# A decoder layer on one core: fixed product order, list turns in two more sequences, a four-bank LayerNorm start, the second norm one group later, and a shared ending

## Chip, cores and metric

The kernel runs on one core of a Trainium2 chip. The metric is the device time of one execution in microseconds (us), the median of several runs; lower is better.

## What is computed

One layer of a decoder over 256 prompt positions and 8 x 4 sample positions, 288 rows in all, which share every weight. In float32, width 2048:

```python
h = rmsnorm(x, norm1_g)
proj = h @ w_in + b_in                     # 2048 -> 3072: a, gate, z
u = a * sigmoid(gate)                      # 1024 channels
c = silu(layernorm(depthwise_causal_conv(u_ext, conv_w, conv_b), ln_g, ln_b))   # 31 taps
d = multiscale_pool(z_ext)                 # 4 groups of 256, windows 2, 4, 8, 16, less z
p = (d @ pool_w, group by group) * pool_scale
x = x + concat[c, p] @ w_out               # 2048 -> 2048
f = square(relu(rmsnorm(x, norm2_g) @ w_ff1))   # 2048 -> 8192
x = x + f @ w_ff2
y = rmsnorm(x, norm_f)                     # also returned: the last 30 u and 15 z of each sequence
```

## The kernel before

Channels lie on the 128 partitions, so a row block is a 128 x 288 tile and x is 16 such tiles (xT). Every weight and every activation is split into a high and a low part of a reduced float32 form, and a product of two blocks is three TensorE products: high x high, weight-low x high, high x activation-low. ScalarE rounds a raw weight tile (wr) to whi (L265, 128 x 1024, a "half" of a block), and the rest, wlo, is made in a way that the table WAYS names for each stage: on VectorE (V, L270), on GpSimd (G, L273), or by an accumulating transfer (D). Five such split tiles are held at once.

gemm (L315) accumulates into PSUM: usually two banks of one 128 x 576 tile (ac, two in use at once), with two k tiles at a time, six products for each bank. 16 k tiles into two banks are 96 products, 8 are 48. The argument classes reorders the head of a gemm: each character asks for the next product in which (k + part) is even or odd. TURN is such a list of 48 characters. between puts small products ahead of a given k tile.

The order of the work: SEQUENCE lists the 16 steps that follow norm 1. c0 to c7 are the column blocks of the convolution (its two gate and value blocks, then sigmoid, then 31 taps on VectorE, L434, at low priority), p3 to p0 the pooled groups (eviction tz L457, window sums on GpSimd, L466 to L475, then dx, L477 and L478), and P3 to P0 the products of a pooled group with its pool_w (tile pp, 12 products), evicted by L489 and L490 into dx again. c0 and c1 run together in four banks; the row sums of norm 1 come near their end, and the row of inverse roots is spread over the partitions in c2. Then come eight W_out column groups over the pooled half (dx), in which the LayerNorm's mean (pmean), sums and row spread are placed, and eight over the convolved half (mx), which ScalarE and VectorE make pair by pair (L564 to L570). After each, x is updated (L559, L580) and the MLP's input ax is made (L596, L597) with its squares summed on GpSimd (ss2, L604). The MLP runs in four chunks: eight groups of w_ff1, eight of w_ff2. Inverse roots come from rsqrt_sums (three one-column products that put row sums on 96 partitions, then steps on 96 x 3 elements) and spread (three products with the identity). At the end the last x tiles are squared and summed the same way, VectorE scales the 16 tiles of xT by the row in six pieces (L652), and SyncE sends each piece out (L653).

The program is written in this order, and a scheduler that models the engines in time orders the instructions of each engine by it; tc.issue_after holds following instructions of the same engine behind a given one. Weights are split one gemm ahead (ready, weights). The lists before the change:

```python
SEQUENCE = "c0 c1 c2 c3 c4 p3 c5 p2 P3 c6 p1 P2 p0 P1 c7 P0"
TURN = "110100" * 4 + "01" * 6 + "1100" * 3
```

TURN is used in c2 (behind 36 alternating places), in the third W_out group of each half, and in the third group of the MLP's first chunk.

## Time and profile before

| | |
|---|---|
| median of 3 runs | 1087.61 us (1087.12 to 1087.72) |
| profiled execution, own time | 1087.97 us |
| its span, first to last instruction | 1086.2 us |
| TensorE / VectorE / ScalarE / GpSimd busy | 99% / 58% / 44% / 17% |
| mean granted TensorE clock | 0.997 |
| HBM read / written | 185.16 MB / 4.28 MB |

The profile comes from one execution. A busy time is the sum over an engine's instructions; PE is TensorE's products, PEld its weight loads, DVE VectorE, ACT ScalarE, POOL GpSimd, SP SyncE. PE also counts products that overlap in the pipeline, and the profile records each product of 288 columns once. The small products with float32 operands are recorded as two.

### The profile page before, as it was taken

Reading aid. Unit: us, or ns where it says so; the run is one execution under the profiler, and the core shown is the slowest. Engines: PE = TensorE matmul, PEld = TensorE weight load, DVE = VectorE, ACT = ScalarE, POOL = GpSimd, SP = SyncE. Lnnn points to the kernel's source line nnn. Section 1 sums busy time; section 2 is a strip of 40 time slices with the busy share of each in tenths; the row PEclk is TensorE's granted clock in tenths of the full one; section 3 lists DMA queues with packets and bytes.
Section 4 is the critical chain, followed back from the end, with each engine's and each line's share of the span. In section 5 each row is a group of like instructions: output and inputs, shape, how many; then the busy total and the mean of one; then the engine's idle time right before and its main releaser. Section 6 shows DMA issues by size and latency. Waiting matters only on the chain.

```text
span 1086.2 us, 19609 instructions
## 1 busy us (share of the span) xinstructions
PE 1073.7 (99%) x8206; PEld 1071.4 (99%) x8206; DVE 634.0 (58%) x813; ACT 477.9 (44%) x583; POOL 182.7 (17%) x212
## 2 busy tenths in 40 slices
PE   9999999999999999999999999999999999999996
PEld 8999999999999999999999999999999999999996
DVE  7899999678555444445454444545544445554553
ACT  8654445475544433334443333444433334444441
POOL 0888989613000000000000000000000000000000
PEclk9999999999999999999999999999999999999998
DMA  9896467545455555555555555555555555555522
GB/s 333 281 269 177 136 178 245 183 153 178 159 171 169 164 172 174 166 167 173 167 167 172 172 165 168 175 167 165 174 169 165 172 173 165 167 174 166 168 76 88
DMA packets 58120, 190.71 MB, mean 176 GB/s; under 512 B 6192, under 2 KB 11312, under 8 KB 58032
## 3 DMA queue, kind: packets, MB, share of 16 engines
q1 hardware_dynamic: 56480, 185.27, 52.2%
q0 software_dynamic: 1008, 3.67, 1.9%
q8 instruction: 64, 1.05, 0.4%
q10 hardware_dynamic: 544, 0.52, 0.1%
q14 instruction: 24, 0.20, 0.0%
HBM read 185.16 MB, written 4.28 MB: 174 GB/s over the span
## 4 chain that ended last, share of the span: by engine, by line
PE 96%; DVE 1%; ACT 1%; DMA 1%; issue 1%; POOL 0%; DVEq 0%
PE ac L315 95%; DMA wr<-in_w 1%; PE pp L315 0%; DVE xT L652 0%; ACT whi L265 0%; DVE wlo L270 0%; POOL wlo L273 0%; PE idle L233 0%; ACT n L567 0%; PE pt L250 0%; PE pt L230 0%; DVE z_all L391 0%; ACT z_all L389 0%; ACT hx L340 0%; DVE n L564 0%
## 5 line engine op out<-in xcount | busy, mean ns | idle before, releaser
L265 ACT CAST whi<-wr 128x1024 fp32r<-128x1024 f32 (+1 forms) x341 | 356.6, 1046 | 558.4 <-PE ac L315 540.4
L270 DVE TENSOR_TENSOR wlo<-wr,whi 128x1024 fp32r<-128x1024 f32 (+1 forms) x295 | 362.9, 1231 | 350.3 <-ACT whi L265 350.3
L315 PE MATMUL ac<-ax,whi 128*128 128x288 f32 x2048 | 351.5, 292 | 0.0
L315 PE MATMUL ac<-fx,whi 128*128 128x288 f32 x2048 | 350.1, 292 | 0.0
L315 PEld LDWEIGHTS ac<-ax,whi 128*128 128x128 f32 x2048 | 296.2, 187 | 0.0
L315 PEld LDWEIGHTS ac<-fx,whi 128*128 128x128 f32 x2048 | 295.6, 187 | 0.0
L315 PE MATMUL ac<-ax,wlo 128*128 128x288 f32 x1024 | 217.4, 292 | 0.0
L315 PE MATMUL ac<-fx,wlo 128*128 128x288 f32 x1024 | 216.3, 292 | 0.0
L315 PEld LDWEIGHTS ac<-ax,wlo 128*128 128x128 f32 x1024 | 162.7, 187 | 0.0
L315 PEld LDWEIGHTS ac<-fx,wlo 128*128 128x128 f32 x1024 | 162.2, 187 | 0.0
L315 PE MATMUL ac<-hx,whi 128*128 128x288 f32 x768 | 136.3, 295 | 0.6 <-DVE hx L338 0.6
L315 PEld LDWEIGHTS ac<-hx,whi 128*128 128x128 f32 x768 | 113.8, 188 | 1.0 <-ACT whi L265 0.8
L273 POOL TENSOR_TENSOR wlo<-wr,whi 128x512 fp32r<-128x512 f32 x78 | 105.9, 1411 | 32.7 <-ACT whi L265 30.4
L434 DVE SCALAR_TENSOR_TENSOR pc<-u_all,vec,pc 128x256 f32<-128x256 f32 x232 | 99.8, 483 | 3.0 <-ACT pc L431 1.6
L315 PE MATMUL ac<-hx,wlo 128*128 128x288 f32 x384 | 86.1, 296 | 0.3 <-DVE wlo L270 0.2
L315 PEld LDWEIGHTS ac<-hx,wlo 128*128 128x128 f32 x384 | 62.7, 188 | 1.1 <-DVE wlo L270 0.9
L315 PE MATMUL ac<-dx,whi 128*128 128x288 f32 x256 | 46.1, 296 | 0.0
L315 PE MATMUL ac<-mx,whi 128*128 128x288 f32 x256 | 45.2, 294 | 0.1
L617 DVE SCALAR_TENSOR_TENSOR t<-ac,r 128x576 f32<-128x576 f32 x32 | 24.2, 758 | 26.3 <-PE ac L315 25.2
L315 PEld LDWEIGHTS ac<-mx,whi 128*128 128x128 f32 x256 | 37.5, 188 | 0.6 <-ACT mx L569 0.3
L315 PEld LDWEIGHTS ac<-dx,whi 128*128 128x128 f32 x256 | 38.0, 188 | 0.1
L646 DVE TENSOR_TENSOR xT<-xT,ac 128x576 f32<-128x576 f32 x24 | 18.1, 754 | 19.4 <-PE ac L315 19.4
(108 smaller groups left out, 502.9 us busy)
## 6 DMA issues: line engine op xcount, KB each, us to landing
wr<-in_w SPq DMA_DIRECT2D x335, 512.0 KB, 3.6
wlo<-in_w POOLq DMA_DIRECT2D x7, 512.0 KB, 7.3
xT<-in_xT SPq DMA_DIRECT2D x7, 288.0 KB, 6.6
out_u_out<-u_all SPq DMA_DIRECT2D x1, 1208.0 KB, 9.7
out_yT<-xT SPq DMA_DIRECT2D x2, 576.0 KB, 2.9
u_all<-in_hist_c SPq DMA_DIRECT2D x8, 136.0 KB, 5.2
wr<-in_w SPq DMA_DIRECT2D x4, 256.0 KB, 3.3
out_z_out<-z_all SPq DMA_DIRECT2D x1, 668.0 KB, 8.2
```

The costliest lines, as they stand in the source:

```text
L265: nc.scalar.copy(hi, raw)
L270: nc.vector.tensor_tensor(lo, raw, f32(hi), op=ALU.subtract)
L273: nc.gpsimd.tensor_tensor(lo[:, j : j + 2, :], raw[:, j : j + 2, :], f32(hi[:, j : j + 2, :]), op=ALU.subtract)
L315: last = nc.tensor.matmul(banks[m][:, :T], gets[k // 8](k % 8, m)[w], rhs[k][x], start=j == ends[m][0], stop=j == ends[m][1])
L434: nc.vector.scalar_tensor_tensor(out=dst, in0=up[:, w : w + SEQ], scalar=cwv[:, w : w + 1], in1=pc, op0=ALU.mult, op1=ALU.add)
L617: nc.vector.scalar_tensor_tensor(out=t, in0=bk[:, :, :T], scalar=0.0, in1=both(r2), op0=ALU.max, op1=ALU.mult)
L646: nc.vector.tensor_tensor(x2, x2, bk[:, :, :T], op=ALU.add)
```

## The change

- **Order.** chain holds the last product; through mm every product from the end of the first gemm up to the third MLP group is issued behind it. P1 moves behind c7. TURN is also used in c5 and c7, and in the second instead of the third W_out group of the first half.
- **Norm 1 and start.** The spread of norm 1's row in c2 stands 12 products later. The first vector transfer goes ahead of x, and the second weight tile is sent after ScalarE's first table load.
- **LayerNorm.** The mean's products stand two k tiles earlier in their group. The first two W_out groups of the second half run as one gemm over four banks, whose two weight blocks are prepared together.
- **Second norm.** Its sums are two products of the split ss2 with a constant matrix, which leave the mean on all partitions; the inverse root is taken on 128 x 288 elements. It stands in the second MLP group instead of behind the first, and the first group is evicted after it.
- **End.** ScalarE takes the root straight from the sums; four VectorE steps follow. The row is spread twice: VectorE scales 12 tiles from the first in PSUM, ScalarE copies the second, and GpSimd scales 4 tiles one by one. Transfers alternate between SyncE and ScalarE.

Lines that are only "..." are left out:

```diff
-SEQUENCE = [(_s[0], int(_s[1])) for _s in "c0 c1 c2 c3 c4 p3 c5 p2 P3 c6 p1 P2 p0 P1 c7 P0".split()]
+SEQUENCE = [(_s[0], int(_s[1])) for _s in "c0 c1 c2 c3 c4 p3 c5 p2 P3 c6 p1 P2 p0 c7 P1 P0".split()]
+TURNS = ("c5", "c7")
...
-        queue.dma_start(raws[-1][:, :, k % 2 : k % 2 + n, :], src[:, :, k % 8 : k % 8 + n, :])
+        queue.dma_start(raws[k // 2][:, :, k % 2 : k % 2 + n, :], src[:, :, k % 8 : k % 8 + n, :])
...
-    for k in range(2):
-        first_weights(k, 1, nc.scalar)
+    first_weights(0, 1, nc.scalar)
+    nc.sync.dma_start(vec[:, 0:NG], io["vec"][:, 0:NG])
...
-        if k == 0:
-            nc.sync.dma_start(vec[:, 0:NG], io["vec"][:, 0:NG])
-        elif k > 1:
+        if k > 1:
...
+    first_weights(1, 1, nc.scalar)
...
-    def rsqrt_sums(parts, scale, after=None, busy=(0, 0)):
+    means = const.tile([P, P], F32R, name="means")
+    nc.vector.tensor_scalar(means, ones, DC / D, None, op0=ALU.mult)
+    cst = const.tile([P, 32], F32, name="cst")
+    eps, mean_d = cst[:, 0:1], cst[:, 1:2]
+    nc.vector.memset(eps, EPS)
+    nc.vector.memset(mean_d, 1.0 / D)
+    def inverse_root(mean, root, y, out):
+        nc.vector.reciprocal(y, root)
+        nc.vector.scalar_tensor_tensor(out=root, in0=mean, scalar=EPS, in1=y, op0=ALU.add, op1=ALU.mult)
+        nc.vector.scalar_tensor_tensor(out=root, in0=root, scalar=-0.5, in1=y, op0=ALU.mult, op1=ALU.mult)
+        nc.vector.scalar_tensor_tensor(out=out, in0=root, scalar=1.5, in1=y, op0=ALU.add, op1=ALU.mult)
+    def rsqrt_sums(parts, scale, after=None):
...
-        idle = cvp.tile([P, 512], F32, name=nm("idle"), tag="cv") if sum(busy) else None
...
-                last = nc.tensor.matmul(pt[:TB, j : j + 1], t[:, j * TB : (j + 1) * TB], ones[:, 0:1], start=n + j == 0, stop=n == len(parts) - 1 and j == 2)
-            with tc.issue_after(last.ins):
-                for j in range(busy[n] if n < 2 else 0):
-                    nc.tensor.matmul(idle[:, 0:P], ones, ones, start=True, stop=True)
+                last = mm(pt[:TB, j : j + 1], t[:, j * TB : (j + 1) * TB], ones[:, 0:1], start=n + j == 0, stop=n == len(parts) - 1 and j == 2)
...
-            last = nc.tensor.matmul(pr[:, j * TB : (j + 1) * TB], s[:, j : j + 1].to_broadcast([TB, P]), ident, start=j == 0, stop=j == 2)
+            last = mm(pr[:, j * TB : (j + 1) * TB], s[:, j : j + 1].to_broadcast([TB, P]), ident, start=j == 0, stop=j == 2)
...
-    def rsqrt_rows(*args):
-        return spread(rsqrt_sums(*args))[0]
...
-    def gemm(banks, rhs, m_outer=False, between={}, classes=""):
+    chain = []
+    def mm(*args, **kw):
+        with tc.issue_after(chain[-1]) if chain else nullcontext():
+            last = nc.tensor.matmul(*args, **kw)
+        if chain:
+            chain[0] = last.ins
+        return last
+    def gemm(banks, rhs, m_outer=False, between={}, classes="", singly=False):
...
-        gets = ready.pop()
-        step = 2 if len(banks) == 2 else 1
-        pairs = [(k, m) for k in range(0, n, step) for m in range(len(banks))]
+        gets = ready.pop(0)
+        units = [(k, 2) for k in range(0, n, 2)]
+        if singly:
+            units = [(k, 1) for k in range(n)]
+        pairs = [(k, width, m) for k, width in units for m in range(len(banks))]
...
-            pairs.sort(key=lambda km: km[1])
-        if step == 2:
-            parts = ((0, 0, 0), (1, 0, 0), (0, 1, 0), (1, 1, 0), (1, 0, 1), (0, 0, 1))
-        else:
-            parts = ((0, 0, 0), (0, 0, 1), (0, 1, 0))
-        todo = [(k + d, m, w, x) for k, m in pairs for d, w, x in parts]
+            pairs.sort(key=lambda p: p[2])
+        parts = {1: ((0, 0, 0), (0, 0, 1), (0, 1, 0)), 2: ((0, 0, 0), (1, 0, 0), (0, 1, 0), (1, 1, 0), (1, 0, 1), (0, 0, 1))}
+        todo, begins = [], {}
+        for k, width, m in pairs:
+            if m == 0:
+                begins[len(todo)] = k
+            todo += [(k + d, m, w, x) for d, w, x in parts[width]]
...
-            if j % (len(banks) * len(parts)) == 0:
-                ahead = between[k]() if k in between else None
-            with tc.issue_after(ahead.ins) if ahead is not None else nullcontext():
-                last = nc.tensor.matmul(banks[m][:, :T], gets[k // 8](k % 8, m)[w], rhs[k][x], start=j == ends[m][0], stop=j == ends[m][1])
+            if begins.get(j) in between:
+                ahead = between[begins[j]]()
+            with tc.issue_after(ahead.ins) if ahead is not None and not chain else nullcontext():
+                last = mm(banks[m][:, :T], gets[k // 8](k % 8, m)[w], rhs[k][x], start=j == ends[m][0], stop=j == ends[m][1])
...
-        for _ in range(8):
+        a, b = split(load()), split(load())
+        yield [lambda k, m: (a, b)[m // 2](k, m % 2)]
+        for _ in range(6):
...
-    with tc.issue_after(gemm(pair0 + pair1, hx, between={15: first_sums})):
-        third = conv_products(2, between={2: first_rows}, classes="01" * 18 + TURN)
+    chain.append(gemm(pair0 + pair1, hx, between={15: first_sums}, singly=True))
+    third = conv_products(2, between={4: first_rows}, classes="01" * 15 + TURN)
...
-            conv_pair(i, conv_products(i))
+            conv_pair(i, conv_products(i, classes=TURN if f"c{i}" in TURNS else ""))
...
-        nc.tensor.matmul(norm["mean"], ones, sum_c[:, 0, :], start=True, stop=False)
-        return nc.tensor.matmul(norm["mean"], ones, cs[-1][:, 1, :], start=False, stop=True)
+        mm(norm["mean"], ones, sum_c[:, 0, :], start=True, stop=False)
+        return mm(norm["mean"], ones, cs[-1][:, 1, :], start=False, stop=True)
...
-    BETWEEN = {5: {4: ln_mean}, 6: {6: ln_sums}, 7: {2: ln_rows}}
-    behind = nullcontext()
+    BETWEEN = {5: {2: ln_mean}, 6: {6: ln_sums}, 7: {2: ln_rows}}
...
-        with behind:
-            last = gemm(each(bk), [mixp[k] for k in korder], between=BETWEEN.get(g, {}), classes=TURN if g == 2 else "")
-        behind = tc.issue_after(last) if g > 3 else nullcontext()
+        gemm(each(bk), [mixp[k] for k in korder], between=BETWEEN.get(g, {}), classes=TURN if g == 1 else "")
...
     for g in range(8):
-        bk = bank2()
-        gemm(each(bk), mixc, classes=TURN if g == 2 else "")
+        if g == 0:
+            joint = [bank2(), bank2()]
+            gemm(each(joint[0]) + each(joint[1]), mixc, classes="01" * 24 + TURN)
+        bk = joint[g] if g < 2 else bank2()
+        if g > 1:
+            gemm(each(bk), mixc)
...
-    r2 = row("r2")
-    ssf = row("ssf")
+    rows2 = []
+    def second_rows():
+        hl = actp.tile([P, 4, T], F32R, name="hl", tag="act")
+        hi, lo = hl[:, 1, :], hl[:, 0, :]
+        nc.scalar.copy(hi, ss2)
+        nc.vector.tensor_tensor(lo, ss2, f32(hi), op=ALU.subtract)
+        bk, r2 = ms("mean2"), row("r2")
+        mean, root = bk[:, 0, :T], bk[:, 1, :T]
+        mm(mean, means, hi, start=True, stop=False)
+        last = mm(mean, means, lo, start=False, stop=True)
+        nc.scalar.activation(root, mean, AF.Sqrt, bias=eps)
+        inverse_root(mean, root, r2, r2)
+        rows2.append(r2)
+        return last
     for ch in range(DFF // FCH):
-        fx = []
+        fx, done = [], []
...
-            gemm(each(bk), x1, classes=TURN if ch == 0 and g == 2 else "")
-            if ch == 0 and g == 0:
-                nc.scalar.copy(r2, rsqrt_rows([ss2], 1.0 / D))
-            t = tmpp.tile([P, 2, T], F32, name=nm("t"), tag="ag", bufs=2)
-            nc.vector.scalar_tensor_tensor(out=t, in0=bk[:, :, :T], scalar=0.0, in1=both(r2), op0=ALU.max, op1=ALU.mult)
-            f = tmpp.tile([P, 2, T], F32, name=nm("f"), tag="ag2", bufs=2)
-            nc.scalar.activation(f, t, AF.Square)
-            fh, fl = act2("fx")
-            nc.scalar.copy(fh, f)
-            nc.vector.tensor_tensor(fl, f, f32(fh), op=ALU.subtract)
-            fx += halves((fh, fl))
+            gemm(each(bk), x1, between={2: second_rows} if ch == 0 and g == 1 else {}, classes="01" * 6 + TURN if ch == 0 and g == 1 else "")
+            if ch == 0 and g == 2:
+                chain.clear()
+            done.append(bk)
+            if ch or g:
+                for bk in done:
+                    t = tmpp.tile([P, 2, T], F32, name=nm("t"), tag="ag", bufs=2)
+                    nc.vector.scalar_tensor_tensor(out=t, in0=bk[:, :, :T], scalar=0.0, in1=both(rows2[0]), op0=ALU.max, op1=ALU.mult)
+                    f = tmpp.tile([P, 2, T], F32, name=nm("f"), tag="ag2", bufs=2)
+                    nc.scalar.activation(f, t, AF.Square)
+                    fh, fl = act2("fx")
+                    nc.scalar.copy(fh, f)
+                    nc.vector.tensor_tensor(fl, f, f32(fh), op=ALU.subtract)
+                    fx += halves((fh, fl))
+                done = []
         last = ch == DFF // FCH - 1
...
+                        ssf = row("ssf")
...
-    rf = rsqrt_rows([ssf, qf], 1.0 / D, None, (3, 6))
-    for k0, n in ((0, 1), (1, 2), (3, 4), (7, 4), (11, 3), (14, 2)):
-        xk = xT[:, k0 : k0 + n, :]
-        nc.vector.tensor_tensor(xk, xk, rf[:, None, :T].to_broadcast([P, n, T]), op=ALU.mult)
-        nc.sync.dma_start(io["yT"][:, k0 : k0 + n, :], xk)
+    ends, again = ms("ends"), cvp.tile([P, 512], F32, name="again", tag="cv")[:, :T]
+    sums_f, rows_f = ends[:TB, 0, 0:3], ends[:, 1, :T]
+    idle = cvp.tile([P, 512], F32, name="idle", tag="cv")
+    for n, (part, busy) in enumerate(((ssf, 3), (qf, 4))):
+        for j in range(3):
+            last = nc.tensor.matmul(sums_f[:, j : j + 1], part[:, j * TB : (j + 1) * TB], mean_d[:, 0:1], start=n + j == 0, stop=n == 1 and j == 2)
+        with tc.issue_after(last.ins):
+            for j in range(busy):
+                nc.tensor.matmul(idle[:, 0:P], ones, ones, start=True, stop=True)
+    root, first, s_f = [cst[:TB, 2 + 3 * j : 5 + 3 * j] for j in range(3)]
+    nc.scalar.activation(root, sums_f, AF.Sqrt, bias=eps[:TB, :])
+    inverse_root(sums_f, root, first, s_f)
+    for spread_f in (rows_f, again):
+        for j in range(3):
+            nc.tensor.matmul(spread_f[:, j * TB : (j + 1) * TB], s_f[:, j : j + 1].to_broadcast([TB, P]), ident, start=j == 0, stop=j == 2)
+    rf = row("rf")
+    queues = (nc.sync, nc.scalar)
+    def finish(eng, r, pieces):
+        for j, (k0, n) in enumerate(pieces):
+            xk = xT[:, k0 : k0 + n, :]
+            eng.tensor_tensor(xk, xk, r[:, None, :].to_broadcast([P, n, T]), op=ALU.mult)
+            queues[j % 2].dma_start(io["yT"][:, k0 : k0 + n, :], xk)
+    finish(nc.vector, rows_f, ((0, 1), (1, 1), (2, 2), (4, 2), (6, 3), (9, 3)))
+    nc.scalar.copy(rf, again)
+    finish(nc.gpsimd, rf, [(k, 1) for k in range(12, KT)])
```

## Prediction

> **What bounds the kernel now.** I read the page first, then the chain of waits, then the time by stage, and the timelines only where stages lose time.
>
> ```profile
> span 1086.2 us, 19609 instructions
> PE 1073.7 (99%) x8206; PEld 1071.4 (99%) x8206; DVE 634.0 (58%) x813; ACT 477.9 (44%) x583; POOL 182.7 (17%) x212
> PEclk9999999999999999999999999999999999999998
> ```
>
> TensorE is busy for 99% of the span at full clock, so time can come only from its start, its end, waits inside, fewer products, or less time for each product. The chain (start, time, what) prices the last of these.
>
> ```profile
> 0.72 4.11 DMA wr<-in_w
> 4.83 0.02 issue
> 4.85 5.33 DMA wr<-in_w
> ...
> 111.40 25.60 PE ac L315 x192
> 137.00 1.60 PE pp L315 x12
> ...
> 284.12 0.43 PE pt L230 x6
> 284.55 5.69 PE ac L315 x42
> 290.24 0.64 PE pt L250 x6
> 290.88 781.06 PE ac L315 x6006
> ```
>
> From 290.88 us on, 6006 products take 781.06 us: 130.05 ns each. From 111.40 us, 192 products of the same shape, unbroken, take 25.60 us: 133.33 ns each. So there are two paces, 3.28 ns apart, and the slow one isn't a wait. Next, the stages. A row counts about two products that reach in from before, so I take two off.
>
> ```profile
> core 0: us, PE busy (x) PEld busy (x) DVE busy (x) ACT busy (x) POOL busy (x), PEclk, DMA share, GB/s
> 48.00:76.00 28.00, 28.00 (x217) 28.00 (x217) 26.11 (x65) 17.00 (x21) 24.45 (x26) 1.00 0.90 255
> 90.00:165.50 75.50, 75.50 (x569) 75.50 (x568) 74.52 (x149) 35.17 (x52) 70.89 (x74) 1.00 0.56 164
> 165.50:188.00 22.50, 22.43 (x169) 22.18 (x169) 21.34 (x44) 12.67 (x16) 22.50 (x22) 1.00 0.80 244
> 188.00:198.00 10.00, 10.00 (x79) 10.00 (x78) 6.04 (x12) 3.16 (x3) 10.00 (x10) 1.00 0.53 164
> 220.70:238.00 17.30, 17.30 (x127) 16.98 (x128) 12.95 (x16) 11.89 (x20) 1.48 (x2) 1.00 0.43 137
> 283.00:306.00 23.00, 23.00 (x179) 23.00 (x178) 12.01 (x17) 11.77 (x14) 0.00 (x0) 1.00 0.48 155
> ```
>
> 48 to 76 us runs at 28.00/215 = 130 ns, 90 to 165.5 us at 75.50/567 = 133 ns, 188 to 198 us at 10.00/77 = 130 ns. Load on the other engines is not the reason: VectorE and GpSimd are busy 93% and 87% of the first stretch too. What precedes the return to 130 ns is the TURN list, an alternation of even and odd products: it stands in sequence c2 (before 48 us) and in the third W_out group, inside the 165.5 to 188 stage. From 90 to 165.5 us no list stands, and the slow pace stays. I read it as a phase of the pipeline that a disturbance tips over and TURN tips back.
>
> **The change part by part.** *TURN in c5 and c7.* Sequences c5, p2, c6, p1, p0 and c7 have 96 products each and P3, P2, P1 and P0 have 12: 624 in all, less 48 in c5 until the list is through. 576 x 3.28 ns = 1.9 us; some stall will tip the phase for part of that, so I take **-1.8**. The list one W_out group earlier saves 48 x 3.28 ns = 0.16 us: **-0.1**.
>
> The Trainium skill, "TensorE: Matmul & The Clock Gate", section "Back-to-back issue gap", gives N / 2.4 + 2.5 ns for a product at full clock, 122.5 ns here (estimate from that page), with no word of order; by it both lists would bring nothing. The trace has 130 and 133 ns for one form at one granted clock, so I go by the trace, and keep the rule as a rival.
>
> *Fixed order; P1 behind c7.* Each product now stands behind the one before it, so TensorE can't fill a wait with products of another group. What is new at one place is that P0, whose input is made by ScalarE, VectorE and GpSimd after sequence p0, stands ahead of the whole W_out part.
>
> ```profile
> 151.57 0.75 DVE L457 TENSOR_TENSOR tz<-ac,rb 128x576 f32<-128x576 f32 x1
> 154.57 1.61 DVE L270 TENSOR_TENSOR wlo<-wr,whi 128x1024 fp32r<-128x1024 f32 x1
> 164.95 0.51 DVE L490 SCALAR_TENSOR_TENSOR dx<-pp,vec,dx 128x288 fp32r<-128x288 f32 x1
> 167.73 1.67 DVE L478 TENSOR_TENSOR dx<-d,dx 128x576 fp32r<-128x576 f32 x1
> 169.65 0.43 PE L315 MATMUL pp<-dx,whi 128*128 128x288 f32 x2
> 160.97 0.42 PE L315 MATMUL pp<-dx,whi 128*128 128x288 f32 x2
> PEld ac L315 <- POOL wlo L273: 0.3, 1, 0.3
> ```
>
> P0 now starts (169.65) as soon as its input is whole (167.73 + 1.67 = 169.40), 17.8 us after p0's eviction begins at 151.57. In the new order only c7 and P1 stand between: (96 + 12) x 0.130 = 14.0 us. As it stands that would be a wait of 3.8 us. Against it: c7's weights move ahead of P1's and are split a quarter of a sequence earlier, so the split at 154.57 (1.61 us) leaves VectorE's queue behind p0; P1's evictions (0.51 at 164.95 and its twin) come after, not before, the last step; together 2.6 us on VectorE, and GpSimd is freed of c7's splits likewise. I take **+0.4**, with ends 0 and +3.8. The wait on GpSimd's split at W_out's start (0.3, last row) should go, since two groups of 12 products now stand before it: **-0.3**.
>
> *LayerNorm's first two groups in four banks.* A pair of input tiles now feeds 24 products (3.1 us) where it fed 12 (1.6 us).
>
> ```profile
> 218.00 1.04 ACT L265 CAST whi<-wr 128x1024 fp32r<-128x1024 f32 x1
> 219.99 1.24 ACT L569 CAST mx<-n 128x576 fp32r<-128x576 f32 x2
> 221.32 1.42 DVE L570 TENSOR_TENSOR mx<-n,mx 128x576 fp32r<-128x576 f32 x2
> L580 DVE TENSOR_TENSOR xT<-xT,ac 128x576 f32<-128x576 f32 x8 | 6.0, 752 | 6.0 <-PE ac L315 5.9
> ```
>
> The first stage of W_out's second half, 220.7 to 238 us, spends 17.30 us on 125 products; at 130.05 ns they are worth 16.26, so 1.0 us is lost. Pairs 2 to 4 then stay ahead of TensorE. The first pair doesn't: its low part ends about 222.0 (half of 1.42 after 221.32), and the fixed order asks for it at the fifth product, 0.5 us after 220.7. Two blocks of weights are now split ahead of the normalization (1.04 us each on ScalarE), so it could come later still. The four banks are both ac tiles, so the third group waits until the first of them is evicted (0.75 us, L580); the joint group's last 12 products (1.6 us) cover that, unless VectorE has just begun a split. Ends: -1.0 and +1.0; I take **-0.4**, near the saving on the later pairs. Moving the mean two steps earlier gives the sums more time, and the later row spread in c2 (12 products, 1.6 us) delays only evictions; TensorE waits for neither in the trace: **0**.
>
> *Second norm in the MLP's second group.* Out go 0.43 and 0.64 us of small products (284.12 and 290.24), in come two products of the common form: 0.26. The stage 283 to 306 us has 165 wide products beside the 12 small ones: 23.00 - 165 x 0.13005 - 1.07 = 0.47 us of slow pace, which shrinks as the list stands a group earlier and no odd shape interrupts. Its inputs are ready long before (sums were asked for only after the first group), and the square root and four VectorE steps over 288 columns, instead of 3,
>
> ```profile
> L490 DVE SCALAR_TENSOR_TENSOR dx<-pp,vec,dx 128x288 fp32r<-128x288 f32 x8 | 4.1, 510 | 0.0
> L237 ACT ACT_TABLE_LOAD x1 | 1.3, 1283 | 0.0
> ```
>
> cost 4 x 0.51 + 1.28 + about 0.4, some 4 us, hidden by the 84 products left of the second group (10.9 us) before a bank is needed. If a reciprocal of 288 columns took three times as long, it would still be hidden. **-1.0** (ends -1.3, -0.6).
>
> *End.* One step (0.16 us, L236) leaves the chain after the last sum. Then the scaling is shared.
>
> ```profile
> L652 DVE TENSOR_TENSOR xT<-xT,pt 128x1152 f32<-128x1152 f32 x2 | 2.6, 1348 | 0.0
> L443 POOL TENSOR_TENSOR sum_c<-sum_c,c 128x288 f32<-128x288 f32 x2 | 1.6, 816 | 0.0
> L236 DVE TENSOR_SCALAR st<-pt 96x3 f32<-96x3 f32 x1 | 0.2, 156 | 1.2 <-PE pt L230 1.2
> 1078.00:1079.00 1.00, 0.00 (x0) 1.00 0.62 235
> 1079.00:1080.00 1.00, 0.00 (x0) 0.92 0.93 382
> 1080.00:1081.00 1.00, 0.00 (x0) 0.50 1.03 410
> 1083.00:1084.00 1.00, 0.00 (x0) 0.50 0.85 327
> ```
>
> VectorE now does 16 tiles at 1.35/4 = 0.34 us each; after, 12 (4.1 us), and GpSimd 4 at about 0.82 (3.3 us, from about 1 us later). But the output, 16 tiles of 128 x 288 x 4 bytes or 2.36 MB, leaves at about 400 GB/s (rows at 1080), so 5.9 us of transfer set the end, and only the slow ramp (235 GB/s at 1078) can be shortened. **-0.6** with the step (ends -0.9, +0.5).
>
> *Start.* One weight transfer now waits for a table load, and the gains come first. The third block's transfer (issued at 4.85, when the first landed at 4.83) sets the chain there, and the same bytes are due ahead of it: **0** (ends -0.6, +0.6, a tenth of the 5.33 us either way).
>
> Sum: -1.8 - 0.1 + 0.4 - 0.3 - 0.4 - 1.0 - 0.6 = **-3.8 us**. The profiled execution took 1087.97 us (span 1086.2 and 1.8 around it) and would take 1084.2; it lies 0.4 above the median of 1087.61, so the prediction is **1083.8**.
>
> **The rivals.** *Slower: P0 blocks TensorE.* Group 1's input took from p1's end (137.00, where P2's products start) to 160.97, 24 us. If P0's took that, TensorE would stand 10 us behind c7 and nothing may pass: 1083.8 - 0.4 + 10 = 1093.4. It is slower by over 0.2% (2.2 us, about what a measurement of this kernel tells from no change) from a wait of 6.4 us on, an input 20.4 us after p0. For it: GpSimd is busy 70.89 of 75.50 us there. Against it: group 0 has one doubling step where group 1 has two, and its 17.8 us contained work that now moves. The granted clock also fell to half about 4 us after the last product (0.92 in the slice from 1079, then 0.50); the same skill page, Part 1, gives an idle window of 3.4 us, and by it such a wait would cost up to 1.7 us more (estimate from that page). Chance 0.13, of which 0.09 slower.
>
> *Order doesn't set the pace*, or new stalls tip it back at once: 1.8 + 0.1 are lost, 1085.7. For it: only two lists stand as witnesses in my rows. Chance 0.12.
>
> *GpSimd's share of the end comes late.* Its copy of the row is made by ScalarE, whose queue now also issues three output transfers that wait for VectorE. Behind the last of them: 4.1 + 0.4 + 3.3 us to the last tile, against 5.9 of transfer, about +2 us: 1085.8. Chance 0.07.
>
> **How the numbers follow.** The forecast has 0.68, all of it faster than 1085.4. The second and third rivals lie on that bound and give 0.08 to faster, 0.11 to no change; the first gives 0.04 to no change and 0.09 to slower. Range: below, the better ends of start, end, LayerNorm and P0, not all at once, 1081.0; above, the two middle rivals and a wait of 3.8 us (1087.2).
>
> **What would show it.** Right: from c5's middle to 160 us products at 130 ns; under 0.5 us between c7's last product and W_out's first beside P1 and P0; no small products at 284 to 291 us; output at 400 GB/s within 1.5 us of its start. Wrong: a gap ahead of the last pp products, 133 ns behind c5, a gap at the fifth product of the four-bank group, or GpSimd's tiles landing last.

## The result: slower, and the profile after

The changed kernel takes 1093.93 us (median of 4 runs, 1093.76 to 1094.74) against 1087.66 for the kernel before in the same session: a ratio of 1.0051, 95% interval 1.0039 to 1.0064, some 6 us slower where 3.8 less were forecast. Its profiled execution took 1094.74 us.

Its page:

```profile
span 1092.9 us, 19605 instructions
PE 1072.3 (98%) x8198; PEld 1069.6 (98%) x8198; DVE 635.4 (58%) x815; ACT 477.2 (44%) x584; POOL 185.5 (17%) x216
PEclk9999998999999999999999999999999999999998
```

The span is 6.7 us longer, yet TensorE is busy for 1.4 us less. The clock row has a new 8 in the seventh of its 40 slices (164 to 191 us), and what TensorE waits for from 100 to 240 us is nearly one thing:

```profile
engine line waited for: us in total, times, longest us
PE pp L302 <- DVE dx L511: 7.5, 1, 7.5
PE ac L302 <- DVE mx L588: 0.6, 1, 0.6
```

pp is the tile of P3 to P0, and the only such wait is the one ahead of P0's first product. TensorE's timeline around it (P1, then P0), and the chain of waits there:

```profile
164.57 0.42 PE L302 MATMUL pp<-dx,whi 128*128 128x288 f32 x2
172.48 0.85 PE L302 MATMUL pp<-dx,whi 128*128 128x288 f32 x2 [7.49 <-DVE dx L511]
...
172.01 0.43 DVE dx L511
172.44 0.04 issue
172.48 3.25 PE pp L302 x12
```

P0's 12 products take 3.25 us, where 12 of this form took 1.60 in the chain of before: the clock was halved while TensorE stood (0.91 on average from 160 to 198 us, below). The stages, first after, then before (columns as in the prediction, down to granted clock, DMA share and GB/s):

```profile
76.00:160.00 84.00, 84.00 (x647) 84.00 (x646) 80.67 (x167) 41.47 (x61) 78.61 (x82) 1.00 0.60 173
160.00:198.00 38.00, 30.51 (x222) 30.28 (x221) 33.62 (x70) 15.42 (x19) 32.67 (x32) 0.91 0.73 208
198.00:238.00 40.00, 39.28 (x294) 38.44 (x293) 23.97 (x33) 23.17 (x31) 13.64 (x11) 1.00 0.47 149
272.00:306.00 34.00, 34.00 (x263) 34.00 (x262) 24.14 (x25) 17.56 (x24) 3.84 (x4) 1.00 0.52 167
```

```profile
76.00:160.00 84.00, 84.00 (x631) 83.87 (x630) 81.83 (x163) 40.51 (x60) 76.58 (x80) 1.00 0.60 172
160.00:198.00 38.00, 37.93 (x288) 37.68 (x287) 32.88 (x69) 18.34 (x22) 38.00 (x36) 1.00 0.74 221
198.00:238.00 40.00, 39.91 (x297) 39.14 (x297) 27.71 (x38) 25.10 (x38) 10.20 (x9) 1.00 0.51 164
272.00:306.00 34.00, 34.00 (x264) 34.00 (x263) 18.89 (x23) 17.20 (x22) 1.92 (x2) 1.00 0.51 164
```

At 0.130 us a product: from 76 to 160 us 16 more products are done (-2.1 us); from 160 to 198, 66 fewer (+8.6); from 198 to 238, 3 fewer (+0.4). From 272 to 306 us before did 12 small products besides the MLP's own, after 2 of the common form, so of the MLP's own before did 252 and after 261: -1.2.

The two ends (the row sums of norm 1 in before and after, from the chains, then the last sums in before and after, from TensorE's timelines):

```profile
30.98 0.43 PE pt L230 x6
32.37 0.43 PE pt L302 x6
1071.78 0.59 PE L230 MATMUL pt<-ones,ssf 128*96 128x1 f32 x6
1079.02 0.59 PE L696 MATMUL ends<-cst,ssf 128*96 128x1 f32 x6
```

The start is 1.4 us later. From the last sums to the span's end before takes 1086.2 - 1071.78 = 14.4 us, after 1092.9 - 1079.02 = 13.9: -0.5. Sum: 1.4 - 2.1 + 8.6 + 0.4 - 1.2 - 0.5 = +6.6 of the span's 6.7.

### The profile page after: what moved, and what is told of

The parts are those of the page before. It is cut to its first block, busy times and chain, and to the rows that moved or that the text cites. A ratio compares the mean times of both kernels' runs of the same rounds, so it can differ in the third digit from the quotient of the medians.

```text
span 1092.9 us, 19605 instructions
## 1 busy us (share of the span) xinstructions
PE 1072.3 (98%) x8198; PEld 1069.6 (98%) x8198; DVE 635.4 (58%) x815; ACT 477.2 (44%) x584; POOL 185.5 (17%) x216
## 4 chain that ended last, share of the span: by engine, by line
PE 70%; issue 20%; DVE 4%; POOL 4%; DMA 1%; ACT 0%; SPq 0%; POOLq 0%; DVEq 0%
PE ac L302 69%; DVE pc L455 2%; POOL wlo L279 2%; POOL s L487 1%; DMA wr<-in_w 1%; DVE wlo L276 1%; DVE dx L499 0%; PE pp L302 0%; POOL prd L459 0%; PE pt L302 0%; POOL xT L713 0%; DVE d L492 0%; DVE dx L511 0%; DVE z_all L412 0%; ACT z_all L410 0%
## 5 line engine op out<-in xcount | busy, mean ns | idle before, releaser
L713 POOL TENSOR_TENSOR xT<-xT,rf 128x288 f32<-128x288 f32 x4 | 3.1, 787 | 800.1 <-ACT rf L717 800.1
L279 POOL TENSOR_TENSOR wlo<-wr,whi 128x512 fp32r<-128x512 f32 x78 | 108.9, 1421 | 39.5 <-ACT whi L271 38.6
L455 DVE SCALAR_TENSOR_TENSOR pc<-u_all,vec,pc 128x256 f32<-128x256 f32 x232 | 98.7, 479 | 2.3 <-ACT pc L452 1.3
```

What stands on the lines that cost most here:

```text
L279: nc.gpsimd.tensor_tensor(lo[:, j : j + 2, :], raw[:, j : j + 2, :], f32(hi[:, j : j + 2, :]), op=ALU.subtract)
L455: nc.vector.scalar_tensor_tensor(out=dst, in0=up[:, w : w + SEQ], scalar=cwv[:, w : w + 1], in1=pc, op0=ALU.mult, op1=ALU.add)
L713: eng.tensor_tensor(xk, xk, r[:, None, :].to_broadcast([P, n, T]), op=ALU.mult)
```

## Experiments

Ratios are to the kernel before in the same session (its median ran from 1087.7 to 1090.7 us between sessions, so ratios are compared, not times). Diffs are against the changed kernel unless said.

**What P0 waits for.** P0 fills the tile that P1 filled before it (there is one pp tile), so it needs two things: its own input, whole at 168.76 + 1.48 = 170.24 us, and P1's result out of the tile, at 172.43. The engines' timelines between P1 and P0 (ScalarE, then VectorE):

```profile
165.98 0.67 ACT L498 CAST dx<-d 128x576 fp32r<-128x576 f32 x1 [1.42 <-POOL d L496]
166.56 0.49 ACT L510 ACTIVATE dx<-pp,vec 128x288 fp32r<-128x288 f32 x1
...
170.70 0.50 ACT L510 ACTIVATE dx<-pp,vec 128x288 fp32r<-128x288 f32 x1 [0.59 <-DVE dx L511]
...
150.22 2.09 DVE L276 TENSOR_TENSOR wlo<-wr,whi 128x1024 fp32r<-128x1024 f32 x1
...
153.02 0.74 DVE L478 TENSOR_TENSOR tz<-ac,rb 128x576 f32<-128x576 f32 x1
...
168.76 1.48 DVE L499 TENSOR_TENSOR dx<-d,dx 128x576 fp32r<-128x576 f32 x1
170.16 0.51 DVE L511 SCALAR_TENSOR_TENSOR dx<-pp,vec,dx 128x288 fp32r<-128x288 f32 x1
...
171.92 0.51 DVE L511 SCALAR_TENSOR_TENSOR dx<-pp,vec,dx 128x288 fp32r<-128x288 f32 x1
```

L510 and L511 evict P1, L498 and L499 make the high and the low part of P0's input, and L478 is the eviction of p0, from which that input starts. P1's eviction stands behind P0's input in both queues, and P0 behind both.

*p0_bank* gives P0 a tile of its own.

```diff
-        bk = ms("pp")
+        bk = bank2() if g == 0 else ms("pp")
```

> The changed kernel, with P0's products in a bank of their own (an ac tile) instead of the one tile that P1 also uses. Theory A (two causes in a row: P0's input whole at 170.2 us, P1's eviction ending at 172.4): only the second falls, 2.2 us less, 1091.7. Rival B (the shared bank alone): the gap goes, about 1085. Rival C (the late input alone): 1093.9 unchanged.

1.0027 [1.0012, 1.0042]. The wait becomes two, P0's high part and then its low part:

```profile
PE ac L302 <- DVE dx L499: 2.8, 1, 2.8
PE ac L302 <- ACT dx L498: 1.7, 1, 1.7
```

4.5 us instead of 7.5, and half clock for 3.4 us instead of 6.8. So the shared tile costs about 3 us; the late input would alone cost 4.5.

*half_taps* takes work off VectorE: in c4 to c7 it leaves out every second tap of the prompt convolution.

```diff
-            for w in range(1, CW):
+            for w in range(1, CW, 1 if i < 4 else 2):
```

> The changed kernel, where the prompt convolution of blocks c4 to c7 takes every second of its taps only (15 steps of 0.43 us each left out, four times, 26 us of VectorE's work). Theory A (P0's input and P1's eviction stand behind VectorE's convolution steps): the gap ahead of P0 falls from 7.7 us to under 3, full clock, about 1086. Rival B (GpSimd's queue and the number of steps set it): the gap stays above 5 us, about 1093.

1.0043 [1.0029, 1.0058], and the wait is still 6.2 us, though VectorE now idles there for 3.4 and 4.2 us at a time. Its releaser is now the input itself, behind GpSimd, whose timeline shows two splits of W_out's weights between the last steps of P0's input (L496 and L496, with one short L495 between the splits):

```profile
164.39 0.71 POOL L496 TENSOR_TENSOR d<-s,z_all 128x32 f32<-128x32 f32 x1
165.07 2.48 POOL L279 TENSOR_TENSOR wlo<-wr,whi 128x512 fp32r<-128x512 f32 x2
...
167.78 2.48 POOL L279 TENSOR_TENSOR wlo<-wr,whi 128x512 fp32r<-128x512 f32 x2
170.22 0.26 POOL L496 TENSOR_TENSOR d<-s,z_all 128x32 f32<-128x32 f32 x1
```

*half_vv* and *full_vv* take those splits off GpSimd, with half and with all taps:

```diff
-... "w": "GG", ...
+... "w0": "VV", "w1": "VV", "w": "GG", ...
```

> The changed kernel with every second tap left out of the prompt convolution in c4 to c7 (15 of 31 steps a sequence, as in half_taps), and W_out's first four weight blocks split on VectorE instead of GpSimd. In half_taps TensorE stood 6.5 us ahead of P0 (164.73 to 171.24) with VectorE idle, and between the three GpSimd steps of P0's input (164.39, 167.53, 170.22) lay two splits of W_out's blocks on GpSimd (two rows of 2.48 us each). Theory, the splits on GpSimd hold P0's input up: without them the three steps follow one another, P0's input is whole some 5 to 8 us earlier, and the gap ahead of P0 falls below 2 us; median about 1089 (ratio 0.999 to 1.001). Rival, the input's own chain (one tile handed between VectorE, GpSimd and ScalarE) takes this long on any queue: the gap stays over 4 us, 1093 to 1094.

> The changed kernel, all taps, with W_out's first four weight blocks split on VectorE instead of GpSimd: 4 splits of about 1.6 us move from GpSimd (5 us each there, in two halves) to VectorE. If GpSimd's splits alone hold P0's input up, the gap of 7.8 us ahead of P0 falls to 2 to 3 us and the median to about 1089. If either engine's queue does as soon as it is full (VectorE is busy with the convolution of c6 and c7 until P0's input is made), the gap stays at 6 to 9 us, with VectorE's splits or convolution steps between the steps of the input: 1092 to 1095.

1.007 [1.0055, 1.0085] and 1.0065 [1.005, 1.008]: moving the splits is no remedy. TensorE waits 8.3 and 7.9 us ahead of P0, and the clock stays at half for 10.24 us in both. The chain of half_vv says why:

```profile
166.32 0.76 DVE dx L499
...
168.38 0.49 ACT dx L510
...
172.30 0.46 DVE dx L511
172.80 3.25 PE pp L302 x12
```

The input is whole at 167.08, 3.2 us earlier than after the change, yet P0 starts at 172.80: now P1's eviction alone ends the wait. Between stand c7's eviction, two rounds of W_out's weights on ScalarE and VectorE and a table load. In full_vv the input is whole at 168.00, P0 starts at 172.13. So after the change two waits end within 2.2 us of each other, and each of these edits only hands the wait to the other. The pair together (a tile of P0's own and the splits moved) wasn't tried.

*filled* keeps TensorE busy with spare products into an unused tile between P1 and P0.

```diff
+            if i == 0:
+                spare = bank2()
+                for _ in range(32):
+                    mm(spare[:, 0, 0:P], ones, ones, start=True, stop=True)
             pool_products(i)
```

> The changed kernel, with 32 spare products of 128 columns, whose result is not used, between P1 and P0, about 6.9 us of work in the 7.7 us gap. Theory A (the idle time halves the clock): the granted clock stays at full and P0's 12 products take 1.6 us, not 2.9; 1.3 us less. Rival B (the half clock costs nothing that the wait doesn't hide): no change, 1093.9.

The clock stays at 1.00 from 160 to 180 us, and P0 isn't slowed:

```profile
172.59 0.53 PE L302 MATMUL pp<-dx,whi 128*128 128x288 f32 x2 [0.42 <-DVE dx L511]
160.00:180.00 20.00, 19.35 (x155) 18.92 (x153) 20.00 (x43) 10.04 (x14) 15.89 (x18) 1.00 0.89 243
```

The median, 1.0037 [1.0022, 1.0051], is in line with that, but its interval overlaps the changed kernel's.

**The order.** *old_p1* puts P1 back ahead of c7 in the fixed order; *p0_early* puts three sequences between p0 and P0; *free_w* lifts the fixed order from P1 to W_out's fifth group; *free_p1* does that with P1 ahead of c7; *free_all* has no fixed order and P1 ahead of c7.

```diff
-p1 P2 p0 c7 P1 P0
+p1 P2 p0 P1 c7 P0          # old_p1, free_p1, free_all
-c5 p2 P3 c6 p1 P2 p0 c7 P1 P0
+c5 p2 P3 p1 p0 P2 c6 P1 c7 P0   # p0_early
+        if (kind, i) == ("P", 1):    # free_w, free_p1
+            chain.clear()
-    chain.append(gemm(pair0 + pair1, ...))        # free_all
+    with tc.issue_after(gemm(pair0 + pair1, ...)):
```

> The changed kernel, fixed order and all, with P1 back ahead of c7. Theory A (under a fixed order each pp block waits for its own input): TensorE stands about 10 us ahead of P1, whose input was whole at 162.1 us while p0 ends at 150.5, and not ahead of P0; about 1096. Rival B (moving P1 behind c7 is what hurts): the gap goes, 1085 to 1087.

> The changed kernel with another fixed order: c0 c1 c2 c3 c4 p3 c5 p2 P3 p1 p0 P2 c6 P1 c7 P0, so that about 25 us of other products lie between each pooled sequence and its own products. Theory A (the price of the fixed order is the short distance from p0 to P0): no gap ahead of any pp product, full clock throughout: 1093.9 - 7.7 - 1.3 - 0.4 = 1084.5 us. Rival B (the backlog of GpSimd and VectorE, not the distance, sets when inputs are whole): the gap moves, ahead of P2, P1 or the LayerNorm's mean, 1088 or above.

> The changed kernel, with the fixed order lifted from P1 to the fifth W_out group. Theory A (the order puts P0, whose input is late and whose bank P1 still holds, ahead of W_out): TensorE fills the 7.7 us gap with W_out products, and P0 runs at full clock, 1.3 us less: 1093.9 - 7.7 - 1.3 = 1084.9 us. Rival B (P1 behind c7 makes the inputs late, whatever the order): W_out's last k tiles need P0, so a gap of 3 us or more stays, 1088 or above.

> The changed kernel with the fixed order lifted from P1 on to W_out's fifth group (as in free_w) and P1 put ahead of c7 again, where the kernel before has it; nothing else. free_w took 1.0025 of the kernel before, free_all, without any fixed order and with P1 ahead of c7, 0.9981. If P1's place behind c7 costs the rest of the wait (P0's bank and the late input), this one comes near free_all: 0.998 to 1.000, about 1087 to 1089, with less than 1.5 us of waiting between 160 and 175 us. If the fixed order up to p0 is what makes the input late, it stays near free_w: 1.002 to 1.003, about 1091, with 3 to 4 us of waiting there.

> The changed kernel without the fixed order: no chain, and P1 ahead of c7 again; lists, four-bank group, second norm, start and end as changed. Theory A (the fixed order is the whole loss; the second norm's 1.5 and the end's 0.5 us are real gains; the pace's gain is given back as a wait on GpSimd at W_out's start, as with the lists alone): 2 us less than the kernel before. Rival B (the start, the four-bank group or the norm cost something too): level with the kernel before, or slower.

| | ratio to before | where TensorE waits | P0 starts, us |
|---|---|---|---|
| as changed | 1.0051 [1.0039, 1.0064] | 7.5 ahead of P0 | 172.48 |
| old_p1 | 1.0061 [1.0046, 1.0076] | 7.3 and 0.8 ahead of P1 | 177.54, no wait |
| p0_early | 1.0028 [1.0015, 1.0041] | 3.4 ahead of the LayerNorm's mean | 165.32, no wait |
| free_w | 1.0025 [1.0015, 1.0035] | 2.6 in W_out, for P1's result | 172.33 |
| free_p1 | 0.9988 [0.9979, 0.9998] | 1.0 in W_out, for low weights | 171.19 |
| free_all | 0.9981 [0.9965, 0.9998] | 1.1 in W_out, for low weights | 170.01 |

In a fixed order the wait moves to whichever input is made too late: P1's, P0's or the last convolution step (chain of p0_early: "204.36 0.49 DVE c L455", then the mean at 204.90). What free_p1 does instead is seen on TensorE's timeline:

```profile
163.13 0.69 PE L302 MATMUL pp<-dx,whi 128*128 128x288 f32 x4
...
164.19 0.30 PE L302 MATMUL ac<-hx,wlo 128*128 128x288 f32 x1
...
171.19 0.43 PE L302 MATMUL pp<-dx,whi 128*128 128x288 f32 x2
...
171.72 0.70 PE L302 MATMUL ac<-dx,whi 128*128 128x288 f32 x4
```

P1's products lie inside c7 (ac from hx) and P0's inside W_out (ac from dx). P0 comes at 171.19, only 1.3 us earlier than in the changed kernel, but nothing stands behind it. Lifting the order where P1 stays behind c7 (free_w) is worth 0.0026; with that, P1's place is worth another 0.0037. With the order fixed, P1's place alone is worth nothing (old_p1: 1.0061, and 1.0051 as changed, with overlapping intervals).

**The terms that were to gain.** *no_lists* takes TURN out of c5 and c7; *before_lists* is the kernel before with nothing but those two lists; *low_last* puts the low parts last among the four-bank group's first 24 products; *old_start* has the start of before.

```diff
-TURNS = ("c5", "c7")
+TURNS = ()                                    # no_lists
-            conv_pair(i, conv_products(i))    # before_lists, against before
+            conv_pair(i, conv_products(i, classes=TURN if i in (5, 7) else ""))
+        if len(banks) == 4 and not singly:    # low_last
+            todo[:24] = sorted(todo[:24], key=lambda p: p[3])
-    nc.sync.dma_start(vec[:, 0:NG], io["vec"][:, 0:NG])   # old_start
+    (vec behind the first x; the second weight tile ahead of the table load)
```

> The changed kernel, without the TURN list in c5 and c7. Theory A (the pace stays 130 ns because no stall tips it any more; the lists themselves cost 0.1 us each): products at 130 ns up to c7, 1093.7. Rival B (my prediction's step: the lists set the pace): 133 ns from 84 us on, 1.8 us more, 1095.7.

1.0068 [1.004, 1.0097]. Without the lists the products of 46 to 163 us still come every 130.0 ns in the profiled execution, so there the lists aren't what keeps the pace: nothing tips it. That execution is the fastest of five (1093.14 us, the others 1093.72 to 1099.85), and no trace shows the pace of the slower ones.

> The kernel before, with TURN lists in c5 and c7 and nothing else changed. Theory A (a list returns the pace to 130 ns): 130 ns from c5's middle to c7 but for new disturbances, 1.8 us less than the kernel before, about 1085.8. Rival B (only the absence of stalls keeps the pace, and without the fixed order something tips it at once): 133 ns stays, 1087.6.

0.9992 [0.9981, 1.0002]: no difference that the median can show. In the trace the pace is gained (76 to 160 us, 16 products more than before, 2.1 us, as after the change), and more than half of it is given back at W_out's start, where the split of the low weights on GpSimd isn't ready (from 160 to 198 us 279 products, 9 fewer than before, 1.2 us):

```profile
76.00:160.00 84.00, 84.00 (x647) 84.00 (x646) 82.26 (x165) 40.99 (x62) 77.58 (x81) 1.00 0.59 173
165.65 0.53 PE L315 MATMUL ac<-dx,wlo 128*128 128x288 f32 x2 [1.28 <-POOL wlo L273]
```

Yet the lists had nothing to repair in this execution either: the pace is 130 ns ahead of c5's list as well. What a list does is seen where the pace is tipped first. In before, the row of two products at 77.80 us takes 0.54 us where its neighbours take 0.42, and the pace is 133 ns from there up to W_out; such a row stands at 74.86 us in old_start, too, and there 133 ns lasts only up to c5's list (before, then old_start ahead of the list and behind it):

```profile
90.00:145.00 55.00, 55.00 (x415) 55.00 (x414) 54.02 (x106) 26.00 (x38) 51.71 (x53) 1.00 0.49 157
75.20:82.00 6.80, 6.80 (x53) 6.77 (x52) 6.78 (x16) 3.38 (x4) 6.21 (x9) 1.00 1.00 294
90.00:145.00 55.00, 55.00 (x425) 55.00 (x424) 52.58 (x107) 26.34 (x39) 52.80 (x53) 1.00 0.50 160
```

With two products taken off for those that reach in, these are 133.2, 133.3 and 130.0 ns each. free_all (tipped at 75.73 us), low_last (78.88) and free_w0v (81.97) return to 130 ns behind the list in the same way.

> The changed kernel, where the four-bank group takes the products with the activation's low part last among its first 24. Theory A (the 0.93 us gap at the fifth product is the wait for the first pair's low part): the gap goes, 0.8 us less, 1093.1. Rival B (the high parts or the weights are as late): 1093.9.

1.0047 [1.0028, 1.0065]: the wait of 0.6 us for mx is gone from the trace, and the stage from 198 to 238 us holds 301 products, 4 more than before and 7 more than after the change; the median can't show so little.

> The changed kernel, with the start's transfers in the old order (second weight tile before the table load, vector behind the first x). Theory A (transfers issued earlier share the bandwidth, so the third block lands 1.4 us later): the first row sums come at 31.0 instead of 32.4 us, 1092.5. Rival B (bandwidth alone sets the start): 1093.9 unchanged.

1.0056 [1.0036, 1.0076]: the median gives nothing back. On TensorE's timeline norm 1's first row sums come at 31.05 us, in before and before_lists at 30.8 and 31.2; in the changed kernel and the sixteen others with its start they come between 31.0 and 35.1, in the middle at 32.1. So the new start seems to cost about 1 us. What is late is the third weight tile, the first of 128 x 1024: after the change ScalarE can round it at 9.56 us, in old_start at 8.43, and only after the change TensorE stands for it:

```profile
10.66 1.06 PE L302 MATMUL ac<-hx,whi 128*128 128x288 f32 x6 [1.38 <-ACT whi L271]
```

In free_p1, relief, old_p1 and free_w0v this wait is longer (1.7 to 2.6 us), the clock stands at half for 3.41 or 6.83 us between 9 and 20 us, and their first sums are the four latest (33.1 to 35.1). In old_start P0 did come 0.8 us earlier (171.72), but the clock stayed at half for 10.24 us instead of 6.83, and W_out's first products paid that back.

**Easing the engines that make P0's input.** *relief* gives half of the splits in c6 to p0 to accumulating transfers; *best* adds p0_early's order and low_last; *free_relief* is free_all with relief's splits; *free_w0v* is free_all with half of W_out's first splits on VectorE.

```diff
-"c": "GGGV", "p": "GVVG"
+"c": "GDGD", "p": "GDDG"        # relief, best, free_relief
-"w": "GG"
+"w0": "GV", "w": "GG"           # free_w0v
```

> The changed kernel, where the late conv and pool weights are split as GDGD and GDDG instead of GGGV and GVVG: half of their low parts come by accumulating transfer, none by VectorE. Theory A (the backlog of VectorE and GpSimd makes P0's input and P1's eviction late): their queues lose some 20 us of work up to 165 us, the gap ahead of P0 shrinks from 7.7 to under 3 us, and the clock holds: 1093.9 - 5 - 1.3 = 1087.6. Rival B (the number of dependent steps from p0 to P0 sets it, not the backlog): the gap stays near 7 us, 1093.

1.0144 [1.0114, 1.0173], the slowest of all. GpSimd is busy for 57.0 of the 75 us from 90 to 165 instead of 71.4, and VectorE for 68.5 instead of 72.6, yet TensorE waits more (5.4, 5.1 and 3.5 us ahead of pp products):

```profile
90.00:165.00 75.00, 65.55 (x471) 64.51 (x470) 68.52 (x143) 38.77 (x51) 57.02 (x67) 0.91 0.77 198
L274 POOL DMA_DIRECT2D wlo<-in_w x15 | 13.1, 876 | 11.9 <-ACT wlo L273 10.3 <-ACT prd L457 1.5
```

The second row (line, operation, count, busy, mean, idle ahead) shows GpSimd idle for 10.3 us ahead of these transfers, waiting for ScalarE's copy; behind each wait stand the steps of the pooled groups. Such a transfer lands 8.9 us after its issue there.

> The changed kernel with the order of p0_early, the low parts last in the four-bank group, and the splits of relief. Theory A: no gap ahead of a pp product, none at LayerNorm's mean (3.8 us in p0_early), none at the fifth product: against p0_early (1092.4) 3.8, half-clock products (0.6) and 0.8 less, about 1086 on this chip, where the kernel before has 1089. Rival B (the backlog isn't shortened by the transfers): the mean's gap stays, 1091.

> free_all with the splits of relief. Theory A (with the backlog gone the pace's 1.5 us is kept too): 3.5 us less than the kernel before. Rival B (W_out's start waits for something else): as free_all.

1.0092 [1.0062, 1.0123] and 1.0094 [1.0065, 1.0124]: TensorE waits 3.7 and 7.7 us for these transfers (in best 6.2 more ahead of pp products).

> free_all, where the second half of W_out's first block is split by VectorE and not by GpSimd. Theory A (the 1.3 us gap at W_out's start is the wait for that half on GpSimd's queue, and it eats the pace's gain): the gap goes, 1.2 us less than free_all, 3 us less than the kernel before. Rival B (VectorE is as late): as free_all, 2 us less than the kernel before.

0.9987 [0.9976, 0.9999], not distinguishable from free_all: the wait at W_out's start goes, and 0.6 and 0.3 us appear ahead of P0 and of the products on P1's result.

## Why the prediction was wrong

**The step that failed** is "Fixed order; P1 behind c7": +0.4 us, ends 0 and +3.8. It measured a wait of 7.5 us and 1.65 more for P0's 12 products at half clock. Four things in it were wrong:

- It had one condition for P0, its input, and took that to be late by 17.8 us less what stands between. The pp tile was not in the sum: with P1 moved next to P0, P1's eviction had to pass between them (p0_bank: some 3 us).
- It counted the 14.0 us of c7 and P1 from the start of p0's eviction. TensorE counts them from p0's last product. In before that is nearly the same (138.60 + 96 x 0.1333 = 151.4, eviction at 151.57); after the change p0's products end at about 138.21 + 96 x 0.130 = 150.7 (138.21: start of p0 on TensorE's timeline), and the eviction starts at 153.02, 2.3 us later, behind the split of 2.09 us on VectorE. So the input came 2.3 + 17.2 - 14.0 = 5.5 us late, and P1's eviction 2.2 us after it; less the 0.3 us until P1's last product ends (164.99), that is the wait to within 0.1 us.
- It credited 2.6 us of work that leaves VectorE's queue between p0 and P0's input. The distance from tz to the whole input went from 17.8 to 17.2 us only (153.02 to 170.24): convolution steps and c7's eviction filled VectorE's time (2.1 us of them between the input's high part, 166.65, and its low part, 168.76), and a split of W_out's weights (162.36, 2.98 us) stood between GpSimd's steps. half_taps and half_vv show that neither queue alone is the cause.
- The halved clock stood only beside the rival, as 1.7 us (an estimate from the Trainium skill, "TensorE: Matmul & The Clock Gate", Part 1). The trace has 3.25 - 1.60 = 1.65, and filled shows that it comes from the standing.

**The rival "P0 blocks TensorE"** had the mechanism and the place. That its time, 1093.4 us, came out too is partly luck: its wait was 10 us where 7.5 came, and the halved clock, the later start and the smaller gains made up for it. Its chance of 0.13 leaned on "17.8 us contained work that now moves". It said "nothing may pass": in free_w, free_p1 and free_all P0 comes at 170 to 172 us just as late, and what differs is whether TensorE may do other products meanwhile.

**The phase term**, -1.9, measured -2.1. The reading behind it is borne out where the pace is tipped: in old_start, free_all, low_last and free_w0v 133 ns lasts up to c5's list and 130 follows it. But in the changed kernel's own execution nothing tips the pace, so there the gain isn't the lists' (no_lists has it as well), and the size is in part luck. Why the row that tips the pace comes in some executions and not in others was not separated. And the gain wasn't free: in before_lists TensorE reached W_out sooner and waited there. The rival "order doesn't set the pace" is not borne out.

**LayerNorm's four banks**, -0.4 within -1.0 and +1.0: the stage gave +0.4. The prediction had named the fifth product as the weak place, and there it stands (0.6 us, for mx). In low_last, without that wait, the stage gives 4 products more than before, -0.5: the saving on the later pairs was there, and the order of the first products took it. Whether the two blocks of weights split ahead of the normalization make mx later was not tried.

**Second norm** -1.0 (ends -1.3, -0.6), measured -1.2: the right mechanism, no small products and no slow pace. **W_out's start** -0.3: no wait for GpSimd's split is left while TensorE comes late; with W_out free to start, 0.2 us of it stand in free_w and 1.0 in free_p1. **End** -0.6, measured -0.5; the output reached 396 GB/s in the third microsecond where 1.5 were forecast. GpSimd's last tile was the last to land, which the prediction had named as a sign of being wrong. It was sent 0.5 us behind VectorE's last piece (1087.59 and 1087.13) and landed 4.4 and 3.6 us after the issue, at 1092.0 and 1090.7; the ending gained even so:

```profile
1086.00:1087.00 1.00, 0.00 (x0) 0.00 (x0) 1.00 (x2) 0.00 (x0) 1.00 (x2) 1.00 1.06 396
...
1087.59 0.58 ACTq L714 DMA_DIRECT2D out_yT<-xT  x1
...
out_yT<-xT ACTq DMA_DIRECT2D x1, 432.0 KB, 3.6
out_yT<-xT ACTq DMA_DIRECT2D x1, 144.0 KB, 4.4
```

**Start** 0 (ends -0.6, +0.6): +1.4 in this execution, about 1 by the traces of all kernels. "The same bytes are due ahead of it" took the start to be bound by bytes; the third weight tile came 1.1 us later than in old_start (9.56 and 8.43). Which of the two moved transfers delays it was not tried.

With the fixed order lifted from P1 on and P1 ahead of c7, the rest of the change is worth 0.0012 of the time, about 1.3 us [0.2, 2.3], where the other terms were to give 4.2: free_p1 still has 278 products in the 38 us from 160 to 198, 10 fewer than before.

```profile
160.00:198.00 38.00, 36.96 (x278) 36.58 (x277) 35.13 (x74) 18.04 (x22) 37.02 (x34) 1.00 0.82 228
```

As in before_lists, TensorE comes to W_out sooner, counted from norm 1's sums (166.18 - 33.42 = 132.8 us, before 165.60 - 30.82 = 134.8), and waits there (1.0 us). free_all and free_p1 are both faster than both kernels, by 0.1 to 0.2% of the kernel before; their intervals overlap, and each only just excludes no difference (upper ends 0.9998).

## What to carry to other kernels

Before fixing an order on the engine that sets the time, list for each stage all that it needs, its output tile's last reader as well as its inputs, and when each is ready in the trace; the order is free only where all of them come early, and otherwise the engine stands where it used to pass on to other work. Where two conditions end close together, relieving one shows nothing: the name of the releaser changes and the time stays. A pace gained ahead of a stage is worth only what that stage's own inputs allow.

## What the runs showed of the hardware

The granted clock fell to half about 4 us after the last product (164.99 to 168.91) and stayed there for 6.83 us; in other runs such stretches were 3.41, 6.83, 10.24 or 13.65 us long, multiples of one window. At half clock a product of 288 columns takes 240 ns. The Trainium skill, "TensorE: Matmul & The Clock Gate", Part 1, gives a free-running window of 3413 ns, and its section "Back-to-back issue gap" N / 1.2 at half clock, 240 ns here (an estimate from that page): the traces agree with both. In free_w waits of 2.6 us and two short ones between 164 and 172 us were enough for one such stretch.

At full clock products of 288 columns kept one of two steady paces, 130.0 or 133.3 ns. In five executions the slower one began ahead of c5's list, at a row of two products with low weights that took 0.50 to 0.54 us instead of 0.42. In the four that have a list in c5 it ended there; in before, which has none, it lasted some 90 us, to W_out.

The accumulating transfers of 512 KB took 7.3 (before) to 8.5 us (relief) from issue to landing, by the medians of the profiles. The Trainium skill, "DMA: Bandwidth & Descriptors", section "Anatomy of one DMA — SWDGE (gpsimd) path", fits 2.0 us + bytes / 436e3, some 3.2 us for 512 KB (an estimate from that page); the traces have more than twice that beside the other transfers, and the measurement decides.
